# A decoder layer in one-level Strassen products: left operands made when their own products come up, branch operands fetched one by one

## The chip, the core and the metric

One core of a Trainium2 chip runs the whole kernel. TensorE (PE) multiplies, VectorE (DVE), ScalarE (ACT) and GpSimd (POOL) do elementwise work, SyncE (SP) issues most DMA transfers. The metric is the device time of one execution in microseconds (us); lower is better. Before the change the median of three runs is 2201.9 us (2199.32 to 2203.22).

## What is computed

One layer on a residual stream h of 1024 tokens by 1024 channels, float32:

```python
f = _swiglu(_rmsnorm(h, ffn1_pre_g), ffn1_w_gate, ffn1_w_up, ffn1_w_down)   # 1024 -> 2816 -> 1024
h = h + 0.5 * _rmsnorm(f, ffn1_post_g)
z = _rmsnorm(h, mix_pre_g) @ w_in                                          # u | v | c | ga | gb
a = u * (causal 128x128 token mixing of layernorm(v))                      # spatial gating unit
b = _pool_mixer(c, pool_w, pool_scale)                                     # trailing means, 4 windows
y = sigmoid(ga) * (a @ w_out_a) + sigmoid(gb) * (b @ w_out_b)
h = h + _rmsnorm(y @ w_o, mix_post_g)
f = _swiglu(_rmsnorm(h, ffn2_pre_g), ffn2_w_gate, ffn2_w_up, ffn2_w_down)
h = h + 0.5 * _rmsnorm(f, ffn2_post_g)
gate = sigmoid(_rmsnorm(h, ple_pre_g) @ ple_w_gate)
h = h + _rmsnorm(gate * (p @ ple_w_proj), ple_post_g)
```

## The kernel before

**Numbers.** A float32 product is done as three products of rounded halves: `split` (L127) makes a high half with a cast on ACT (L128) and a low half with a subtraction on DVE (L129); `mm3` (L134) issues low x high (L136), high x low (L137) and high x high (L138). One matmul instruction is 128x128 by 128x512.

**Strassen.** Every large product is cut into 2x2 blocks and done with seven products instead of eight, in the order p1, p2, p5, p6, p3, p7, p4. Left operands 0 and 1 (for p1, p2) are plain blocks; 2 to 6 are sums of blocks or the block a22. `Seven` (L167) holds a left operand's seven versions; `put` splits one piece into its place, `sums` (L177) makes operands 2, 6 and 3 in a step `first` and 5 and 4 in a step `second`, with half tiles from a pool of four (`half`, L99) for its intermediate sums. `feed` (L197) does this from normalised rows: tokens t = 0 to 3 give operands 0 and 1 (`early`), tokens 4 to 7 the rest (`late`), each after eight transposes on TensorE (L209). `FromDram` and `SumsFromDram` (L238, L273) read a left operand, or its ready sums, from DRAM.

**Stages**, in order: projection of p (to 49 us); first FFN's gate and up products (to 479), its down product (to 709); v of the mixer with its token mixing (to 812); u and c (to 985); gates, with the pooling products among them (to 1155); branch a (to 1233); branch b (to 1312); output projection (to 1401); second FFN (1412 to 2081); gate of the layer embedding, PLE (to 2181); final norm and output. `Columns` (L400) runs the groups of output columns, `Rows` (L485) the products whose output is by tokens, `ffn_down` (L644) the down products. `Columns` with `lead` = 2 runs p1 and p2 of the first two groups ahead of everything else, since operands 0 and 1 are ready first; then each group's other products. Weights come through `Right` (L334), made three steps ahead. Raw tiles from DRAM come from a pool of six (`raw`), full tiles from a pool of eleven (`full`).

**Order of side work.** `Later` (L39) is a queue of postponed steps with keys and costs: after each half product `allow(us)` pops steps while credit lasts; `flush` pops all. `closing` (L678) finishes a product's rows: squares on ACT (L149), scale on POOL (L143, L144), residual on DVE (L704), a second norm (L159), and then `feed`. `down_sums` (L572) makes sums of the next down product's weights in half tiles and stores them; `weight_sums` (L807) does that for the mixer's output weights, beside the first down product (`beside`). `sgu_constants` (L844) loads, masks (L852, on POOL) and transposes (L858) the token weights in the mixer's v stage. Branch outputs are multiplied by their gates and summed in DRAM: a's are written to `y_d`, b's are added there by an accumulating DMA from POOL's queue (L1067), and the output projection reads `y_d` as its left operand. The Tile framework's scheduler sets the final order of each engine's instructions from the order of the program and its own estimates; engines then run their rows in that order.

Of the kernel before, what the change touches and what calls it, by code (L numbers as in the profile page):

```python
# [38 lines left out]
class Later:  # L39

    def __init__(self):
        self.queue, self.credit, self.count = [], 0.0, 0

    def add(self, key, cost, step):
        heapq.heappush(self.queue, (key, self.count, cost, step))
        self.count += 1

    def allow(self, us):  # L50
        self.credit = min(self.credit + us, us)
        while self.queue and self.credit > 0:
            self.pop()

    def pop(self):
        _, _, cost, step = heapq.heappop(self.queue)
        self.credit -= cost
        step()

    def flush(self):  # L60
        while self.queue:
            self.pop()
# [3 lines left out]
def layer_kernel(ctx: ExitStack, tc: tile.TileContext, a: dict, out: bass.AP):  # L66
# [46 lines left out]
    ga_d, gb_d, c_d = (scratch(s, KD) for s in ("ga_", "gb_", "c_"))  # L113
    b_d, y_d = (dr.tile([P, KD, T], F32, name=s, tag=s) for s in ("b_d", "y_d"))
    as_d = scratch("a_s", 7, KD // 2 * HT)

    tw_d = {s: [scratch(f"{s}_t{h}", 4) for h in range(2)] for s in ("w_out_a", "w_out_b", "w_o")}
    sv_d = dr.tile([P, KD, T], F32, name="sv_d", tag="sv_d")
# [47 lines left out]

    class Seven:  # L167
        def __init__(self):
            self.op, self.kept = [None] * 7, {}

        def put(self, i, k, cols, src, e=nc.vector):
            if self.op[i] is None:
                self.op[i] = X([2, 4, HT], FR)
            o = self.op[i]
            split(o[:, 0, k, cols], o[:, 1, k, cols], src, e)

        def sums(self, k, cols, a11, a12, a21, a22, tmp):  # L177

            s2 = tmp()

            def first():
                s1 = tmp()
                nc.vector.tensor_tensor(s1, a22, a21, op=ALU.subtract)
                self.put(2, k, cols, s1)
                self.put(6, k, cols, a22)
                nc.vector.scalar_tensor_tensor(s2, a11, -1.0, s1, op0=ALU.mult, op1=ALU.subtract)
                self.put(3, k, cols, s2)

            def second():
                nc.vector.tensor_tensor(a21, a11, a21, op=ALU.subtract)  # L190
                self.put(5, k, cols, a21, nc.vector)
                nc.vector.scalar_tensor_tensor(s2, a12, -1.0, s2, op0=ALU.mult, op1=ALU.subtract)
                self.put(4, k, cols, s2)

            return first, second

        def feed(self, src, t, key):  # L197
# [3 lines left out]
            state = []  # L201
# [18 lines left out]
            def tmp():  # L220
                return half().rearrange("p (j t) -> p j t", j=4)

            def late():
                banks = transposed()
                a21 = tmp()
                nc.scalar.copy(a21, banks[0])
                a1, a2 = self.kept[t - 4][:, 0], self.kept[t - 4][:, 1]
                first, second = self.sums(k, cols, a1, a2, a21, banks[1], tmp)
                first()
                state.append(second)  # L230

            if t < 4:
                later.add(key, 1.4, early)
            else:
                later.add(key, 3.5, late)
                later.add(key, 2.8, lambda: state.pop()())

    class FromDram(Seven):  # L238
# [11 lines left out]
        def early(self):  # L250
            for kk in range(2):
                for i in range(2):
                    self.put(i, slice(2 * kk, 2 * kk + 2), slice(0, HT), self.block(0, i, kk))

        def late(self, kks, key):
            def one(kk):
                state = []

                def begin():
                    a11, a12, a21, a22 = (self.block(r, c, kk) for r in range(2) for c in range(2))  # L260
                    first, second = self.sums(
                        slice(2 * kk, 2 * kk + 2), slice(0, HT), a11, a12, a21, a22, lambda: full((2, HT))
                    )
                    first()
                    state.append(second)

                later.add(key, 6.2, begin)
                later.add(key, 4.9, lambda: state.pop()())

            for kk in kks:  # L270
                one(kk)

    class SumsFromDram(Seven):  # L273


        def __init__(self, src):
            Seven.__init__(self)
            self.src = src

        def load(self, i, kk):  # L280
            t = raw([2, HT])
            nc.sync.dma_start(t, self.src[i][:, kk * D:(kk + 1) * D].rearrange("p (k t) -> p k t", k=2))
            self.put(i, slice(2 * kk, 2 * kk + 2), slice(0, HT), t)

        def early(self):
            for i in range(2):
                for kk in range(2):
                    self.load(i, kk)

        def late(self, key):  # L290
            for i in range(2, 7):
                for kk in range(2):
# [870 lines left out]
```

## Time and profile before

| | |
|---|---|
| median of three runs | 2201.9 us |
| the profiled execution | 2197.74 us |
| its span | 2196.0 us |
| TensorE clock, mean | 0.975 of full |
| DMA | 421.67 MB, mean 192 GB/s |
| VectorE instructions | 1773 |
| GpSimd's queue (accumulating DMA) | 2304 packets, 4.20 MB |

A row of a profile view names line, engine, operation and tiles, `out<-in`; brackets hold the idle time ahead of it on its engine and what ended it. Lines are those of the kernel before. In the views, "x" is a count of instructions.

### The profile page before, as it was taken

What the parts mean: (1) busy time and instruction counts of PE and PEld (TensorE: products, weight loads), DVE (VectorE), ACT (ScalarE), POOL (GpSimd) and SP (SyncE); (2) the same over time, 40 slices, a digit from 0 to 9 for tenths busy, and PEclk for the clock granted to TensorE, in tenths of its full rate; (3) what the DMA queues carried; (4) which work ended last, traced back from release to release, by engine and by line L of the source; (5) the groups of instructions that cost most, each with busy time, mean ns of one, the idle gap of its engine ahead of it and who ended that gap; (6) DMA issues with size and microseconds to landing.
All of it is one profiled execution on the core that took longest, in us unless ns stands there. A gap on an engine that the chain in (4) does not pass through costs nothing. (4 is left out here: it accounts for less than half of the span.)

```text
span 2196.0 us, 25524 instructions
## 1 busy us (share of the span) xinstructions
PE 2084.6 (95%) x9228; PEld 1718.0 (78%) x9228; DVE 1472.1 (67%) x1773; ACT 944.0 (43%) x1359; POOL 141.8 (6%) x224
## 2 busy tenths in 40 slices
PE   7899999999999999999999998679999999999985
PEld 6688888888877788888788886568888888888774
DVE  6756666686575896567665757876666667545586
ACT  7433333344265633335454435643333334444463
POOL 2000000000012110000000012300000000001112
PEclk9999999999999999999999999889999999999998
DMA  8453545489866236445468887544354456764635
GB/s 286 141 172 120 190 137 168 158 306 385 357 223 203 73 111 203 138 154 161 133 227 296 271 229 225 197 141 162 135 169 157 146 180 225 230 194 164 205 118 192
DMA packets 300622, 421.67 MB, mean 192 GB/s; under 512 B 20048, under 2 KB 176720, under 8 KB 300496
## 3 DMA queue, kind: packets, MB, share of 16 engines
q1 hardware_dynamic: 298192, 415.84, 56.2%
q0 software_dynamic: 2304, 4.20, 1.2%
q8 instruction: 73, 1.20, 0.2%
q14 instruction: 53, 0.43, 0.1%
HBM read 286.27 MB, written 133.69 MB: 191 GB/s over the span
## 5 line engine op out<-in xcount | busy, mean ns | idle before, releaser
L136 PE MATMUL ps<-X,wt 128*128 128x512 f32 x1904 | 744.9, 392 | 22.9 <-ACT X L128 17.5
L137 PE MATMUL ps<-X,wt 128*128 128x512 f32 x1904 | 745.0, 391 | 1.9 <-DVE X L129 1.9
L138 PE MATMUL ps<-X,wt 128*128 128x512 f32 x1904 | 742.3, 391 | 0.0
L129 DVE TENSOR_TENSOR wt<-raw,wt 128x1024 fp32r<-128x1024 f32 x282 | 344.4, 1222 | 231.1 <-ACT wt L128 230.9
L136 PEld LDWEIGHTS ps<-X,wt 128*128 128x128 f32 x1904 | 359.8, 189 | 99.7 <-ACT X L128 18.6
L137 PEld LDWEIGHTS ps<-X,wt 128*128 128x128 f32 x1904 | 359.8, 189 | 78.0 <-DVE X L129 3.3
L138 PEld LDWEIGHTS ps<-X,wt 128*128 128x128 f32 x1904 | 359.8, 189 | 75.0
L128 ACT CAST wt<-raw 128x1024 fp32r<-128x1024 f32 x282 | 295.7, 1050 | 276.2 <-PE ps L138 158.1
L129 DVE TENSOR_TENSOR X<-raw,X 128x1024 fp32r<-128x1024 f32 (+1 forms) x198 | 222.3, 1146 | 148.4 <-ACT X L128 142.4
L128 ACT CAST X<-raw 128x1024 fp32r<-128x1024 f32 (+1 forms) x198 | 190.9, 992 | 177.0 <-PE ps L138 40.2
L136 PE MATMUL ps<-X 128*128 128x512 f32 x616 | 236.2, 394 | 9.1 <-ACT X L128 9.0
L137 PE MATMUL ps<-X 128*128 128x512 f32 x616 | 241.9, 393 | 1.3 <-DVE X L129 1.3
L138 PE MATMUL ps<-X 128*128 128x512 f32 x616 | 240.7, 392 | 0.0
L132 DVE TENSOR_TENSOR raw<-raw 128x1024 f32<-128x1024 f32 x136 | 165.9, 1222 | 9.9 <-DMA raw<-in_ple_w_gate_dram 3.0
L136 PE MATMUL ps<-wt,X 128*128 128x512 f32 x336 | 134.0, 412 | 12.5 <-ACT wt L128 9.4
L136 PEld LDWEIGHTS ps<-X 128*128 128x128 f32 x616 | 116.7, 190 | 34.6 <-ACT X L128 10.4
L137 PE MATMUL ps<-wt,X 128*128 128x512 f32 x336 | 135.4, 403 | 4.4 <-DVE wt L129 4.4
L137 PEld LDWEIGHTS ps<-X 128*128 128x128 f32 x616 | 116.8, 190 | 26.4 <-DVE X L129 2.2
L138 PEld LDWEIGHTS ps<-X 128*128 128x128 f32 x616 | 116.8, 190 | 24.4
L138 PE MATMUL ps<-wt,X 128*128 128x512 f32 x336 | 134.2, 400 | 0.0
L323 ACT ACTIVATE f<-ps 128x512 f32<-128x512 f32 x88 | 52.3, 598 | 126.0 <-PE ps L138 126.0
L321 ACT ACTIVATE f<-ps 128x512 f32<-128x512 f32 x88 | 52.4, 598 | 100.3 <-PE ps L138 96.4
(128 smaller groups left out, 1863.3 us busy)
## 6 DMA issues: line engine op xcount, KB each, us to landing
raw<-ffn_s SPq DMA_DIRECT2D x70, 512.0 KB, 5.2
raw<-in_ffn_w_gate_dram SPq DMA_DIRECT2D x96, 256.0 KB, 4.1
raw<-in_ffn_w_up_dram SPq DMA_DIRECT2D x96, 256.0 KB, 4.6
f<-in_ffn_w_down_dram SPq DMA_DIRECT2D x44, 512.0 KB, 4.9
ffn_t<-hf SPq DMA_DIRECT2D x88, 256.0 KB, 4.8
ffn_s<-hf SPq DMA_DIRECT2D x88, 256.0 KB, 4.9
raw<-ffn_t SPq DMA_DIRECT2D x40, 512.0 KB, 4.8
ffn_s<-f SPq DMA_DIRECT2D x66, 256.0 KB, 2.0
```

The source lines that it names most:

```text
L128: nc.scalar.copy(hi, src)
L129: e.tensor_tensor(lo, src, hi.bitcast(F32), op=ALU.subtract)
L132: e.tensor_tensor(dst, u, v, op=ALU.add)
L136: nc.tensor.matmul(ps, wl[1], wr[0], start=first, stop=False, skip_group_check=True)
L137: nc.tensor.matmul(ps, wl[0], wr[1], start=False, stop=False, skip_group_check=True)
L138: nc.tensor.matmul(ps, wl[0], wr[0], start=False, stop=last, skip_group_check=True)
L321: nc.scalar.activation(at("22"), y, AF.Copy, scale=-1.0)
L323: nc.scalar.activation(at("12"), x, AF.Copy, scale=-1.0)
```

## The change

Left operands 3, 4 and 5 are no longer made with 2 and 6. The arithmetic and the splits for p6, p3 and p7 are bound to their product and forced only when that product comes up (`before`, `meet`, `need`); until then they run when credit allows. The sums are made in place, in tiles kept anyway and in one more operand tile (`rest`), not in half tiles:

```diff
+    def before(self, product, cost, step):
+        self.due.append((product, self.count, 0, cost, step))
...
+    def meet(self, product):
+        while self.due and self.due[0][0] <= product:
+            self.pop(self.due)
...
-        def sums(self, k, cols, a11, a12, a21, a22, tmp):
...
+        def sums(self, k, cols, a11, a12, a21, a22, s1, us):
+            nc.vector.tensor_tensor(s1, a22, a21, op=ALU.subtract)
+            self.put(2, k, cols, s1)
+            self.put(6, k, cols, a22)
+
+            def others():
+                nc.vector.scalar_tensor_tensor(s1, a11, -1.0, s1, op0=ALU.mult, op1=ALU.subtract)
+                self.put(3, k, cols, s1)
+                nc.vector.scalar_tensor_tensor(a12, a12, -1.0, s1, op0=ALU.mult, op1=ALU.subtract)
+                nc.vector.tensor_tensor(a11, a11, a21, op=ALU.subtract)
+
+            later.before(self.base + 3, 4 * us, others)
+            later.before(self.base + 4, us, lambda: self.put(4, k, cols, a12))
+            later.before(self.base + 5, us, lambda: self.put(5, k, cols, a11))
...
-                a21 = tmp()
+                if t == 4:
+                    self.rest = X([2, 4, HT], F32)
+                a21, s1 = (self.rest[:, i, :, cols] for i in range(2))
```

Both branches read ready sums, one operand (two loads of 512 KB) at a time, started in the last products of the stage ahead; b's sums are now made where the pooling products end, and both branches run without `lead`. Gates are read and multiplied two blocks at a time; in b's second group a's part of y is loaded and added on DVE, and two blocks of y go into the output projection's operands straight from SBUF:

```diff
+        def fetch(self):
+            i, self.fetched = self.fetched, self.fetched + 1
+            for kk in range(2):
+                t = raw([2, HT])
+                nc.sync.dma_start(t, self.src[i][:, kk * D:(kk + 1) * D].rearrange("p (k t) -> p k t", k=2))
...
+    def last_a(i):
+        if i >= 2:
+            left_b.fetch()
+        if i == 6:
+            b_cols.right.ahead(2)
...
+    def done_b(g, key, where, o):
+        if g == 0:
+            nc.gpsimd.dma_start(y_d[:, where[0], where[1]], o, accum_op=ALU.add)
+            return
+        ya = raw([2, HT])
+        nc.sync.dma_start(ya, y_d[:, where[0], where[1]])
+        add(o, o, ya)
...
+    def last_b(i):
+        if i == 4:
+            ysum.early(0)
+        if i == 5:
+            o_rows.right.ahead(1)
+        if i == 6:
+            later.add(0, 3.7, lambda: ysum.late(0))
```

Other work is placed elsewhere: the token weights are masked and transposed in the projection of p, stored and read back (`token_weights`); `down_sums` runs after a group instead of ahead of it; the next stage's loads start at p4 of a down product instead of p7; the sums of the mixer's output weights are spread over its first five products; closing norms may wait a few half products; and weights are made two steps ahead, not three, in the first three steps of an FFN:

```diff
+    def token_weights():
+        ws, turned = half(), half()
+        w = ws.rearrange("p (g s) -> p g s", g=SGU_G)
+        nc.sync.dma_start(w, a["sgu_w"][0].rearrange("g t s -> t g s"))
...
+        nc.sync.dma_start(ws_d, turned)
...
-            if i == 5:
-                last()
...
-                if kp % 2 == 0 and beside:
+                if beside and (kp == 1 or (i, kp) == (0, 3)):
                     beside.pop(0)()
+
             rest = [right.get(i * PAIRS + kp) for kp in range(outer, PAIRS)]
+            if i == 6:
+                last()
...
-            later.add(t + 1, 1.3, norm)
-            left.feed(hp, t, t + 2)
+            later.add(t + 1, 1.3, norm, 1)
+            left.feed(hp, t, t + 2, max(3, t))
...
-            self.right = Right(make, self.steps, 3)
+            self.right = Right(make, self.steps, lambda s: LOOK if s < 2 * lead - 1 else 3)
...
-            self.right = Right(lambda i: make(i, state, (True, False)), list(range(7)), 1)
+            self.right = Right(lambda i: make(i, state, (False, False)), list(range(7)), 1)
```

How this moves instructions, at three places. (Rows are line, operation, `out<-in` with tile numbers, and shape. In the changed kernel `split` is L147 and L148, the norm L178, the sums L207 to L215, the residual L730.)

VectorE ahead of the first FFN's first p5, whose left operand is X_514 and whose weight is wt_762. Before:

```order
L192 SCALAR_TENSOR_TENSOR hf_745<-f_418,hf_745 128x512
L132 TENSOR_TENSOR f_853<-f_853,ps_901 128x512
L129 TENSOR_TENSOR wt_917<-raw_758,wt_917 128x1024
L132 TENSOR_TENSOR hf_834<-hf_831,f_826 128x512
L132 TENSOR_TENSOR hf_837<-f_824,f_826 128x512
L605 TENSOR_TENSOR f_822<-f_822,f_853 128x512
L129 TENSOR_TENSOR X_561<-hf_745,X_561 128x4x128
L183 TENSOR_TENSOR hf_868<-ps_860,hf_865 128x512
L190 TENSOR_TENSOR hf_865<-f_459,hf_865 128x512
L186 SCALAR_TENSOR_TENSOR hf_867<-f_459,hf_868 128x512
L129 TENSOR_TENSOR X_514<-hf_868,X_514 128x4x128
```

After, where the same operand is X_513, its last piece is written here, and 67 matmul rows follow before p5 reads it:

```order
L212 SCALAR_TENSOR_TENSOR X_510<-f_419,X_510 128x4x128
L148 TENSOR_TENSOR wt_732<-raw_729,wt_732 128x1024
L148 TENSOR_TENSOR X_513<-X_510,X_513 128x4x128
L214 SCALAR_TENSOR_TENSOR f_355<-f_355,X_510 128x512
L215 TENSOR_TENSOR f_355<-f_355,X_510 128x512
L148 TENSOR_TENSOR X_516<-ps_653,X_516 128x4x128
```

The last token's difference (L183), the two sums behind it and the sums of down weights (hf_834, hf_837) stood ahead of the operand's last piece; now one weight and another token's scaled sum do.

VectorE between token 5's residual (L704, L730) and its normalised row (L159, L178), in the seam from the output projection to the second FFN. Before:

```order
L704 SCALAR_TENSOR_TENSOR f_10166<-f_10166,sc_10641,raw_10638 128x1024
L692 TENSOR_TENSOR f_10181<-ps_9980,f_10052 128x512
L192 SCALAR_TENSOR_TENSOR hf_10609<-f_10312,hf_10609 128x512
L129 TENSOR_TENSOR wt_10800<-raw_10793,wt_10800 128x1024
L704 SCALAR_TENSOR_TENSOR f_10181<-f_10181,sc_10663,raw_10660 128x1024
L132 TENSOR_TENSOR hf_10736<-f_10732 128x512
L129 TENSOR_TENSOR X_10679<-hf_10609,X_10679 128x4x128
L159 SCALAR_TENSOR_TENSOR raw_10638<-f_10166,sc_10671,f_10054 128x1024
```

After:

```order
L730 SCALAR_TENSOR_TENSOR f_10107<-f_10107,sc_10578,raw_10575 128x1024
L207 TENSOR_TENSOR X_10653<-ps_10648,X_10653 128x4x128
L151 TENSOR_TENSOR raw_10774<-raw_10774,raw_10777 128x1024
L148 TENSOR_TENSOR X_10656<-X_10653,X_10656 128x4x128
L178 SCALAR_TENSOR_TENSOR raw_10575<-f_10107,sc_10586,f_10001 128x1024
```

Token 6's residual, token 4's last sum and split and a down-weight sum are gone from between; a weight sum and token 4's operand 2 stand there.

SyncE's loads from branch b's end into the output projection (`y_d` is the gated sum, `gb_d` the gates, `in_w_o` and `w_o_t` the weights of the output projection). Before:

```order
L247 DMA raw_9895<-y_d_138 128x2x512
L247 DMA raw_9897<-y_d_138 128x2x512
L247 DMA raw_9899<-y_d_138 128x2x512
L247 DMA raw_9901<-y_d_138 128x2x512
L501 DMA raw_9932<-in_w_o_dram 128x2x512
L501 DMA raw_9934<-in_w_o_dram 128x2x512
L247 DMA raw_9995<-y_d_138 128x2x512
L247 DMA raw_9997<-y_d_138 128x2x512
L247 DMA raw_9999<-y_d_138 128x2x512
L247 DMA raw_10001<-y_d_138 128x2x512
L493 DMA raw_10028<-w_o_t00_162 128x1024
```

After:

```order
L1097 DMA raw_9863<-gb_d_130 128x2x512
L266 DMA raw_9867<-y_d_131 128x2x512
L266 DMA raw_9869<-y_d_131 128x2x512
L266 DMA raw_9871<-y_d_131 128x2x512
L266 DMA raw_9873<-y_d_131 128x2x512
L1121 DMA raw_9896<-y_d_131 128x2x512
L522 DMA raw_9899<-in_w_o_dram 128x2x512
L522 DMA raw_9901<-in_w_o_dram 128x2x512
L514 DMA raw_9975<-w_o_t00_162 128x1024
```

The weights of p2 (the first two rows of `in_w_o`) stood behind four loads of y; now behind five and a load of gates, and the next weights directly follow.

More of the change, by code (lines that the diff above doesn't have):

```diff
@@ L164, in gain @@
         return g
+    ALL = slice(0, HT)
+    count = [0]
     class Seven:
@@ L248, in block, with early, late @@
             return out
[L250 to L271, printed above, removed]
+        def early(self, kk):
+            for i in range(2):
+                self.put(i, slice(2 * kk, 2 * kk + 2), ALL, self.block(0, i, kk))
+        def late(self, kk):
+            a21, a22, a11, a12 = (self.block(r, c, kk) for r in (1, 0) for c in range(2))
+            self.sums(slice(2 * kk, 2 * kk + 2), ALL, a11, a12, a21, a22, full((2, HT)), 1.3)
     class SumsFromDram(Seven):
@@ L277, in __init__, with need @@
             Seven.__init__(self)
[L278 to L292, printed above, removed]
-                    later.add(key, 1.3, lambda i=i, kk=kk: self.load(i, kk))
+            self.src, self.fetched = src, 0
+        def fetch(self):
[3 more added lines that the diff above has]
+                nc.sync.dma_start(t, self.src[i][:, kk * D:(kk + 1) * D].rearrange("p (k t) -> p k t", k=2))
+                k = slice(2 * kk, 2 * kk + 2)
+                later.before(self.base + i, 1.3, lambda t=t, k=k: self.put(i, k, ALL, t))
+            later.first = True
+        def need(self, i):
+            if self.fetched < 7:
+                self.fetch()
+            later.meet(self.base + i)
     def pairs():
@@ L305, in pairs, with packed, places, at @@
         return at
+    def packed():
+        tiles = {}
+        def places(n):
+            def at(key):
+                if key not in tiles:
+                    tiles[key] = full((2, HT))
+                return tiles[key][:, n, :]
+            return at
+        return tiles, places(0), places(1)
     class Out:
@@ L342, in get @@
         def get(self, s):
[L343 removed]
+            self.ahead(s + 1 + self.look(s))
             out, self.done[s] = self.done[s], None
@@ L605, in up @@
                 nc.vector.tensor_tensor(g[key], g[key], src, op=ALU.mult)
-            return [Out(gate, places), Out(up)]
+            return [Out(gate, places), Out(up, others)]
         def after(c):
             spill(hid.pop(c), lambda i: s_d[s][i][:, c * HT:(c + 1) * HT])
+            if c < HC - 1:
+                down_sums(c)
+            if c == HC - 2:
+                down_sums(c + 1)
             if c == HC - 1:
                 later.flush()
-        cols.run(left, outs, after, last)
+        cols.run(left, outs, after, lambda i: last() if i == 6 else None)
     PAIRS, TAIL = (HC + 1) // 2, 2
@@ L943, in uc_outs @@
         return [Out(u_final, u_places), Out(c_final, c_places)]
-    uc_cols.run(left, uc_outs, lambda g: None, lambda: gate_cols.right.ahead(2), 5)
+    uc_cols.run(left, uc_outs, lambda g: None, lambda i: gate_cols.right.ahead(2) if i == 6 else None, 5)
     later.flush()
@@ L1012, in products @@
             w, blk = state["w"], 2 * gi + b
+            both = full((2, HT))
             for h in range(2):
@@ L1073, in layer_kernel, with branch, outs, one @@
-    o_rows = Rows(a["w_o"][0], tw_d["w_o"])
-    def last_a():
-        b_cols.right.ahead(2)
-        left_b.early()
-    def last_b():
-        o_rows.right.ahead(1)
-        ysum.early()
-        ysum.late((0,), 0)
-    a_cols.run(left_a, outs_a, lambda g: None, last_a)
-    left_b.late((0, 1), 0)
-    b_cols.run(left_b, outs_b, lambda g: None, last_b)
-    ysum.late((1,), 0)
+    gate_cols.run(left, gate_outs, lambda g: None, gate_last, 25, 1.0)
+    def branch(gates, done):
+        def outs(g):
+            tiles, *places = packed()
+            gts = {}
+            def one(n):
+                def f(key, src):
+                    h, c = int(key[0]) - 1, int(key[1]) - 1
+                    where = (slice(4 * c + 2 * g, 4 * c + 2 * g + 2), slice(h * HT, (h + 1) * HT))
+                    if n == 0:
+                        gts[key] = raw([2, HT])
+                        nc.sync.dma_start(gts[key], gates[:, where[0], where[1]])
+                    if key == "21":
+                        nc.vector.tensor_tensor(places[n](key), src, gts[key][:, n], op=ALU.mult)
+                    elif n == 1:
+                        nc.vector.tensor_tensor(tiles[key], tiles[key], gts[key], op=ALU.mult)
+                    if n == 1:
+                        done(g, key, where, tiles[key])
+                return Out(f, places[n])
+            return [one(0), one(1)]
+        return outs
@@ L1090, in layer_kernel @@
+    later.add(0, 3.7, lambda: ysum.sums(slice(2, 4), ALL, *(tops[i] for i in range(4)), full((2, HT)), 1.3))
     h2_cols = hidden_weights("ffn2")
```

179 lines of the change are left out of this document (85 added, 94 removed).

## The prediction

> **What bounds the kernel now.** I read the profile's page first, then TensorE's waits, then stretches of time, then single stretches of the timeline.
>
> ```profile
> PE 2084.6 (95%) x9228; PEld 1718.0 (78%) x9228; DVE 1472.1 (67%) x1773; ACT 944.0 (43%) x1359; POOL 141.8 (6%) x224
> PE   7899999999999999999999998679999999999985
> PEclk9999999999999999999999999889999999999998
> ```
>
> TensorE is busy for 95% of the span, so at most 111 us of idle time can go (2196.0 - 2084.6), plus what a lowered clock costs. Both sit in few places: the slices of 54.9 us that aren't 9 are the first two, the 25th to 27th (1318 to 1482 us, from the mixer's output projection into the second FFN) and the last two. What stands before TensorE there:
>
> ```profile
> PE ps L136 <- ACT X L128: 26.5, 5, 9.1
> PE ps L209 <- DVE raw L159: 25.8, 8, 8.6
> PE ps L136 <- ACT wt L128: 10.2, 5, 4.1
> PE ps L858 <- POOL hf L852: 2.9, 1, 2.9
> ```
>
> (us in all, times, longest.) Three quarters are waits for a left operand's high half (L128 into X), for the normalised rows that are transposed (L159 before L209), or for a weight. None of it is a shortage over the whole span: VectorE (DVE) has 67%. It is order, at seams where VectorE has norms, operand sums and weights to do at once. By stretches:
>
> ```profile
> 60.00:100.00 40.00, 29.13 (x118) 22.84 (x117) 28.34 (x40) 17.31 (x26) 0.00 (x0) 0.87 0.46 151
> 200.00:250.00 50.00, 50.00 (x222) 41.42 (x221) 31.45 (x37) 16.85 (x22) 0.00 (x0) 1.00 0.42 137
> 1300.00:1350.00 50.00, 42.75 (x166) 33.74 (x165) 36.68 (x40) 20.73 (x29) 10.23 (x9) 0.90 0.88 250
> 1400.00:1470.00 70.00, 41.59 (x174) 33.47 (x173) 59.89 (x80) 35.69 (x64) 13.61 (x19) 0.78 0.54 179
> 2075.00:2120.00 45.00, 37.47 (x170) 29.76 (x169) 39.62 (x51) 26.47 (x49) 14.50 (x18) 0.96 0.38 128
> 814.00:817.00 3.00, 3.00 (x11) 2.61 (x11) 2.83 (x9) 2.07 (x2) 0.00 (x0) 0.50 0.66 198
> ```
>
> (Length, then busy time and count of PE, PEld, DVE, ACT, POOL, then granted clock, DMA share, GB/s.) The undisturbed stretch from 200 on gives the price of a 128x512 matmul: 50.00/222 = 0.225 us. By it the 118 rows of 60 to 100 are worth at most 26.6 us; there are 10.9 us of idle time and at least 2.6 us of slow clock. In 1400 to 1470, 28.4 us are idle and at least 2.4 us (41.59 - 174 x 0.225) go to the clock, while VectorE is busy for 86%.
>
> **The change, part by part.** Instruction counts on PE and VectorE are the same in both programs, so this is a change of places. I used one tool for all parts: between two rows of TensorE's order I added the VectorE rows at the distance from start to start of these
>
> ```profile
> 1456.17 0.68 DVE L129 TENSOR_TENSOR X<-hf,X 128x512 fp32r<-128x512 f32 x1
> 1456.77 0.68 DVE L129 TENSOR_TENSOR X<-ps,X 128x512 fp32r<-128x512 f32 x1
> L129 DVE TENSOR_TENSOR wt<-raw,wt 128x1024 fp32r<-128x1024 f32 x282 | 344.4, 1222 | 231.1 <-ACT wt L128 230.9
> L128 ACT CAST wt<-raw 128x1024 fp32r<-128x1024 f32 x282 | 295.7, 1050 | 276.2 <-PE ps L138 158.1
> ```
>
> (0.60 us for 512 columns; for 1024 the 1.22 shown less the same overlap, 1.14), and compared with 24 matmuls, 5.4 us. What VectorE has above TensorE in such a slice I call its excess. Checked on before: 9.9 us of excess ahead of the first p5, against 10.9 idle; 36.4 in the seam of 1400 to 1470, against 28.4. So it finds the places, and overstates seams by about a fifth.
>
> *1. Operand sums late (first FFN).* Now the p5 product waits for the last token's operands:
>
> ```profile
> 83.39 1.22 PE L136 MATMUL ps<-X,wt 128*128 128x512 f32 x2 [8.37 <-ACT X L128]
> 84.03 0.69 DVE L186 SCALAR_TENSOR_TENSOR hf<-f,hf 128x512 f32<-128x512 f32 x1 [0.62 <-DMA ffn_t<-hf]
> ```
>
> and L186 itself waits for a half tile that a transfer to `ffn_t` holds. In the order of after, operand 2 is complete 67 matmul rows (15 us) ahead of p5, there are no half tiles in the way, and the sums of down weights stand behind the group. The 10.9 us and 2.6 us go: -13.5. Late next: the transposes of tokens 6 and 7 are moved up among the projections of p, where the slices carry 4.5 us more excess than before. Net **-9** (from -13.5 to -3).
>
> *2. Same part at the second FFN, with the closing norm's order.* Here are three long waits and one chain:
>
> ```profile
> 1411.07 1.94 PE L209 MATMUL ps<-ident,raw 128*128 128x128 f32 x8 [8.56 <-DVE raw L159]
> 1427.77 1.94 PE L209 MATMUL ps<-ident,raw 128*128 128x128 f32 x8 [8.44 <-DVE raw L159]
> 1459.36 1.22 PE L136 MATMUL ps<-X,wt 128*128 128x512 f32 x2 [9.10 <-ACT X L128]
> 1419.88 1.28 DVE L704 SCALAR_TENSOR_TENSOR f<-f,sc,raw 128x1024 f32<-128x1024 f32 x1
> 1421.19 1.06 ACT L149 ACTIVATE raw<-f 128x1024 f32<-128x1024 f32 x1 [0.77 <-DVE f L704]
> 1423.63 2.67 POOL L144 TENSOR_TENSOR sc<-sc,nhalf 128x1 f32<-128x1 f32 x1
> 1426.34 1.29 DVE L159 SCALAR_TENSOR_TENSOR raw<-f,sc 128x1024 f32<-128x1024 f32 x1 [0.44 <-POOL sc L144]
> ```
>
> From token 5's residual (L704) to its transposes (1427.77) is a chain of 7.9 us that no order shortens below its own steps. What the order changes is when L704 starts: before, it stands behind ten VectorE rows, most of them sums and splits of token 4; after, it is the first row behind token 4's transposes. Excess of the seam falls from 36.4 to 21.9; scaled by 28.4/36.4 that is -11.3, and I add -1 for slow clock. **-12** (from 0, if the chain binds in all four tokens, to -25).
>
> *3. The next norm's seam (PLE).* Same rules, but there the excess rises from 13.0 to 17.7. The stretch 2075 to 2120 has 7.5 us idle; 4.7 x 7.5/13.0 = **+3** (-3 to +6).
>
> *4. Token weights.*
>
> ```profile
> 729.77 1.30 POOL L852 TENSOR_SCALAR_AFFINE_SELECT hf<-hf 128x512 f32<-128x512 f32 x1 [0.25 <-DMA hf<-in_sgu_w_dram]
> 731.12 0.66 PE L858 MATMUL ps<-ident,hf 128*128 128x128 f32 x4 [2.90 <-POOL hf L852]
> ```
>
> Both move to the prologue, behind a norm that TensorE waits for anyway; later only a load remains, beside other work. **-3** (-4 to 0). If that cover isn't there, the 1.3 us of the select are paid at the start.
>
> *5. The down products' ends.*
>
> ```profile
> 661.83 2.08 PE L136 MATMUL ps<-X 128*128 128x512 f32 x4 [4.13 <-ACT X L128]
> 2033.93 2.07 PE L136 MATMUL ps<-X 128*128 128x512 f32 x4 [3.86 <-ACT X L128]
> 605.32 0.51 PE L136 MATMUL ps<-X 128*128 128x512 f32 x1 [1.01 <-ACT X L128]
> 606.58 0.50 PE L137 MATMUL ps<-X 128*128 128x512 f32 x1 [0.75 <-DVE X L129]
> 609.15 0.50 PE L137 MATMUL ps<-X 128*128 128x512 f32 x1 [0.58 <-DVE X L129]
> ```
>
> The first two are p7's operands, with the next stage's loads ahead of them on SP's queue; those loads now stand after p4's. The last three follow a stretch in which the sums for `w_o` and the branches' weights share the DMA with down's operands; they are spread over five products now. Gone: 8.0 + 2.3, and 2 of slow clock. New: 3.9 us of excess where p4 begins in the first down product, 3.1 more than before in the second; if they are paid in full, 7. **-5** (-10 to +5).
>
> *6. Branches and output projection.* Operands one by one: in the order each load is issued at least 28 us ahead of its product, against 6.1 us to land, so the fetches cost nothing; what hides them is the five products (5.4 us each) that run between an operand's load and its use. The first weight of a and of b is issued only 6.3 us ahead:
>
> ```profile
> raw<-a_s SPq DMA_DIRECT2D x14, 512.0 KB, 6.1
> raw<-in_w_o_dram SPq DMA_DIRECT2D x6, 512.0 KB, 5.8
> raw<-in_w_out_a_dram SPq DMA_DIRECT2D x6, 512.0 KB, 4.9
> 1324.65 1.20 PE L136 MATMUL ps<-wt,X 128*128 128x512 f32 x4 [3.66 <-ACT wt L128]
> 1066.30 0.64 PE L136 MATMUL ps<-X,wt 128*128 128x512 f32 x1 [2.43 <-DVE wt L129]
> ```
>
> it needs 4.9 + 1.05 + 1.22 = 7.2, so 0.9 of wait, twice, for the 2.4 us of 1066. In the output projection before, a weight issued 3.4 us (15 matmul rows) ahead waited 3.66; 1300 to 1350 has 7.25 us idle. After, p2's weight is issued only 1.8 us (8 rows) ahead, because gate and `y` tiles hold the raw buffers: 5.8 + 1.05 - 1.8 = 5 us, then two lesser waits of 1 to 2.5 us. **0** (-6 to +6).
>
> Sum: -9 - 12 + 3 - 3 - 5 + 0 = **-26 us**, against the profiled execution, 2197.7 us (span 2196.0): 2171.7. The median of the runs, 2201.9, is 4.2 us above that execution; on its scale the sum gives **2176**.
>
> The slow clock counts in two of these terms, and the trace shows it after short waits too:
>
> ```profile
> 811.72 0.33 PE L136 MATMUL ps<-f,raw 128*128 128x128 f32 x1 [1.84 <-DVE raw L886]
> ```
>
> after 1.84 us of idle time the stretch 814 to 817 ran at 0.50. [...]
>
> **Rivals.**
> - *The norm's chain binds* (chance 0.15). The four tokens' transposes wait 7.9 us each whatever VectorE does between; part 2 gives 0, and the output projection's late weights cost 4. For it: L159 ends just before both transposes. Against: before L704 VectorE was never free. -26 + 12 + 4 = -10: 2192.
> - *The waits move from p5 to p6; slower* (0.11). Four VectorE rows per token (0.69 each in 512 columns, 2.75) are now due when p6 comes up; five operands are made so, four tokens each: 5 x 4 x 2.75 = 55 us. It decides where VectorE is still behind when p5 ends, since p6's steps are then forced in one block that p5's 5.4 us can't hide. In full: -26 + 55 = +29: 2231; half of it still ends at 2204. For it: in the order at the second FFN p6's last operand is finished right before p6. Against: at the first FFN it stands some 50 rows ahead.
> - *It does nothing measurable* (0.06): gains of parts 1 and 2 are given back at p4 of down and at PLE; 2200.
> - *All seams clear* (0.10): parts 1 to 5 at their good ends, -45 or more: 2157.
>
> **How the numbers follow.** The forecast has 0.58; its own range is 2160 to 2193, from the parts' bounds taken as independent. For 8 in 10 the range takes in the first and third rival, the better end of "all seams clear", and the milder half of p6's: **2150 to 2206**. A measurement of this kernel tells 0.2% (4.4 us) from no change. Faster by more: 0.58 less a little, 0.10 and most of 0.15: 0.78. Within: 0.09. Slower: 0.13.
>
> **What would show it.** Part 1: no wait over 2 us ahead of the first p5. Part 2: 1400 to 1470's counterpart with some 17 us idle, not 28. Part 4: no wait for the select. Part 5: no 4 us at p7's operands. Part 6: a wait of about 5 us for p2's weight in the output projection. Wrong if p6, p3 or p7 products wait for X in the FFNs, or if branch products wait for their operands' loads.

## The result, and the profile after

| | before | after |
|---|---|---|
| median of four runs | 2202.4 us | 2148.3 us |
| range | 2199.3 to 2203.2 | 2148.0 to 2153.8 |
| profiled execution, its span | 2197.7, 2196.0 | 2153.8, 2151.7 |

Ratio of after to before: 0.9763, 95% interval 0.9744 to 0.9781, so 48 to 56 us less. The forecast was 26, and the median lies 1.7 us below the lower end of the range given with it (2150 to 2206). The profile of after is of its slowest run: its span is 44.3 us shorter than that of before, its three other runs were another 5.5 us shorter.

The page of after, the lines shown of before:

```profile
PE 2070.9 (96%) x9228; PEld 1712.7 (80%) x9228; DVE 1472.0 (68%) x1773; ACT 939.9 (44%) x1360; POOL 141.0 (7%) x212
PE   7999999999999799999999999989999999999986
PEclk9999999999999899999999999999999999999988
```

VectorE has the same work (1472.1 before). TensorE's busy time fell by 13.7 us for the same matmuls (its mean clock rose from 0.975 to 0.983), and its idle time by 30.6. The slices at 1318 to 1482 us are nines but one; one slice has become worse, the 14th (700 to 750 us). TensorE's waits of after:

```profile
PE ps L232 <- DVE raw L178: 35.3, 11, 7.2
PE ps L155 <- DVE f L345: 4.7, 3, 2.4
PE ps L155 <- ACT X L147: 2.6, 1, 2.6
PE ps L156 <- DVE wt L148: 2.3, 4, 1.0
PE ps L155 <- ACT wt L147: 0.8, 1, 0.8
```

Waits for a left operand's high half have gone from 26.5 to 2.6 us, those for a weight's cast from 10.2 to 0.8. Waits of transposes for the normalised rows (L232 for L178) have grown from 25.8 to 35.3. By stretches, in the columns used above: the first FFN's first products, the output projection, the seam into the second FFN, the seam into PLE, and the one into v:

```profile
60.00:100.00 40.00, 40.00 (x178) 33.15 (x177) 34.28 (x44) 21.64 (x31) 0.00 (x0) 1.00 0.34 105
1276.00:1326.00 50.00, 48.80 (x215) 39.76 (x214) 41.31 (x42) 25.41 (x35) 2.00 (x2) 1.00 0.75 251
1375.00:1445.00 70.00, 57.41 (x242) 46.44 (x241) 62.19 (x79) 39.27 (x66) 10.07 (x15) 0.88 0.42 132
2030.00:2075.00 45.00, 32.59 (x139) 26.08 (x138) 38.81 (x51) 25.44 (x48) 12.69 (x16) 0.85 0.41 141
695.00:735.00 40.00, 27.77 (x114) 22.48 (x113) 34.22 (x45) 21.69 (x38) 10.08 (x10) 0.83 0.38 118
```

The first is full, with 178 matmuls where before had 118 in it. The output projection's idle time went from 7.25 to 1.2 us, that of the FFN's seam from 28.4 to 12.6, but PLE's rose from 7.5 to 12.4.

To compare whole stages I took, in both traces, the time from the m-th to the n-th of the 9228 recorded matmuls. Both programs have the same number of matmuls in nearly the same order, so I take a difference in such a stretch as that stage's gain:

| stretch (matmuls) | term of the prediction | forecast | before to after | measured |
|---|---|---|---|---|
| first FFN's start (60 to 300) | 1 | -9 | 70.6 to 56.4 | -14.2 |
| into the second FFN (5760 to 6240) | 2 | -12 | 137.4 to 121.6 | -15.8 |
| into PLE (8760 to 9060) | 3 | +3 | 74.9 to 82.0 | +7.1 |
| v stage (2880 to 3180, 3180 to 3600) | 4 | -3 | 74.4 to 82.2, 80.0 to 76.3 | +4.1 |
| down products (2500 to 2640, 2640 to 2880, 8580 to 8700) | 5 | -5 | 35.3 to 31.7, 57.6 to 58.6, 30.1 to 23.5 | -9.2 |
| gates to a (4560 to 5040), b into output projection (5640 to 5760) | 6 | 0 | 115.3 to 114.9, 39.6 to 29.0 | -11.0 |
| PLE's end (9060 to 9227) | none | 0 | 48.2 to 40.3 | -7.9 |

They add up to -46.9; behind the last matmul after takes 2.8 us longer.

Each value is from one profile. Between seams the profiles agree closely (matmuls 300 to 2500 take 498.7 us in all of them), but at the seams they scatter, and the profile of after is on the slow side: its 114.9 us for gates to a holds a wait of 2.4 us with a granted clock of 0.50 behind it, and the eleven edits of the changed kernel below take 110.9 to 112.9 there. Where a difference of a few us matters below, the spread over the runs is given.

### The profile page after: what moved, and what is told of

Same layout as the page of the kernel before. It is cut to its first block, busy times and chain, and to the rows that moved or that the text cites. A ratio compares the mean times of both kernels' runs of the same rounds, so it can differ in the third digit from the quotient of the medians.

```text
span 2151.7 us, 25497 instructions
## 1 busy us (share of the span) xinstructions
PE 2070.9 (96%) x9228; PEld 1712.7 (80%) x9228; DVE 1472.0 (68%) x1773; ACT 939.9 (44%) x1360; POOL 141.0 (7%) x212
## 5 line engine op out<-in xcount | busy, mean ns | idle before, releaser
L148 DVE TENSOR_TENSOR wt<-raw,wt 128x1024 fp32r<-128x1024 f32 x282 | 343.5, 1220 | 235.0 <-ACT wt L147 234.9
L147 ACT CAST wt<-raw 128x1024 fp32r<-128x1024 f32 x282 | 295.5, 1050 | 268.7 <-PE ps L157 129.2
L148 DVE TENSOR_TENSOR X<-raw,X 128x1024 fp32r<-128x1024 f32 (+1 forms) x201 | 224.0, 1145 | 113.6 <-ACT X L147 113.1
L147 ACT CAST X<-raw 128x1024 fp32r<-128x1024 f32 (+1 forms) x201 | 192.1, 993 | 156.2 <-PE ps L157 66.6
L156 PE MATMUL ps<-wt,X 128*128 128x512 f32 x336 | 133.8, 398 | 1.8 <-DVE wt L148 1.8
L155 PE MATMUL ps<-wt,X 128*128 128x512 f32 x336 | 132.1, 401 | 1.2 <-DVE f L345 1.2
L157 PE MATMUL ps<-wt,X 128*128 128x512 f32 x336 | 133.0, 396 | 0.0
L340 ACT ACTIVATE f<-ps 128x512 f32<-128x512 f32 x88 | 52.6, 598 | 122.5 <-PE ps L157 122.3
```

Of the source, the lines that this page charges most:

```text
L147: nc.scalar.copy(hi, src)
L148: e.tensor_tensor(lo, src, hi.bitcast(F32), op=ALU.subtract)
L155: nc.tensor.matmul(ps, wl[1], wr[0], start=first, stop=False, skip_group_check=True)
L156: nc.tensor.matmul(ps, wl[0], wr[1], start=False, stop=False, skip_group_check=True)
L157: nc.tensor.matmul(ps, wl[0], wr[0], start=False, stop=last, skip_group_check=True)
L340: nc.scalar.activation(at("12"), x, AF.Copy, scale=-1.0)
```

## The experiments

Each is an edit of the changed kernel or of the one before, timed against before on the same chip. "Ratio" is to before throughout; the changed kernel's is 0.9763 (0.9744 to 0.9781).

**Are the late operands what pays?** The changed kernel with operands made at once:

```diff
-            later.before(self.base + 3, 4 * us, others)
-            later.before(self.base + 4, us, lambda: self.put(4, k, cols, a12))
-            later.before(self.base + 5, us, lambda: self.put(5, k, cols, a11))
+            others()
+            self.put(4, k, cols, a12)
+            if cols is ALL:
+                self.put(5, k, cols, a11)
+                return
+            self.last5 = getattr(self, "last5", []) + [lambda: self.put(5, k, cols, a11)]
+            if len(self.last5) == 4:
+                for step in self.last5:
+                    step()
...
-                later.add(key, 2.1, late, wait)
+                later.add(key, 6.3, late, wait)
```

> The changed kernel, but operands 3 and 4 and their sums are made at once with 2 and 6 again (operand 5 with the last token's), in place as in the change. If the lateness of the sums pays (terms 1 and 2 of the prediction, -13 and -16 us in the trace): waits of 6 us or more come back ahead of p5 in both FFNs, and the time rises by 15 to 30 us over the changed kernel, to 2163-2178. If it is the half tiles and the moved sums of down weights that cleared p5: no wait over 3 us ahead of p5, 2146-2154.

Measured: 2148.3 us, ratio 0.9760 (0.9741 to 0.9778). With the other parts of the change in place, lateness, which gives the change its name, is worth nothing in the total that could be told from zero (the intervals leave some 6 us either way). Ahead of the first p5 there is no wait, as in the stretch of 60 to 100 us:

```profile
60.00:100.00 40.00, 40.00 (x183) 33.20 (x182) 35.16 (x45) 19.09 (x29) 0.00 (x0) 1.00 0.31 95
```

It isn't that nothing moves. At once, the seam into v (matmuls 2880 to 3180) takes 75.9 us instead of 82.2 (77.8 to 82.2 in the ten runs with late sums there) and the one into PLE 78.1 instead of 82.0 (78.5 to 82.1 in nine runs), but the rest of the v stage (3180 to 3600) takes 85.7 instead of 76.3 (76.3 to 76.4 in the ten), with waits of 1.5 and 2.8 us for the centred rows of v, and the seam into the second FFN 122.6 instead of 121.6. Gains and losses cancel.

**Is it the sums of down weights?** The kernel before, with this one part of the change:

```diff
-            later.add(0, 1.4, first)
-            later.add(0, 1.4, lambda: state.pop()())
+            later.add(90, 1.4, first)
+            later.add(91, 1.4, lambda: state.pop()())
...
-            down_sums(c)
...
+            if c < HC - 1:
+                down_sums(c)
+            if c == HC - 2:
+                down_sums(c + 1)
```

> The kernel before, with one part of the change: the sums of the next down product's weights run after a group instead of ahead of it. If half tiles held by their transfers delayed the operand sums: the 8.4 us wait ahead of the first p5 falls below 4, and the time falls by 5 to 15 us, to 2187-2197. If the operand sums themselves are too much for VectorE there: the wait stays over 6, and the time stays within 4 us of 2202.

Measured: 2180.5 us, ratio 0.9912 (0.9896 to 0.9929), 19 us less: more than either theory allowed for. The first p5's wait hasn't halved, it has gone, with the operand sums, the half tiles and everything else as before:

```profile
60.00:100.00 40.00, 40.00 (x183) 33.20 (x182) 32.91 (x42) 18.65 (x26) 0.00 (x0) 1.00 0.29 90
```

Matmuls 60 to 300 take 56.1 us (70.6 before, 56.4 changed), so this part is the whole of term 1. The seam into the second FFN goes from 137.4 to 133.0, with the two waits of transposes still there and the one of 9.1 us for operands cut to two of 2.2:

```profile
1397.13 1.09 PE L209 MATMUL ps<-ident,raw 128*128 128x128 f32 x4 [8.75 <-DVE raw L159]
1412.31 1.09 PE L209 MATMUL ps<-ident,raw 128*128 128x128 f32 x4 [9.71 <-DVE raw L159]
1439.02 0.73 PE L136 MATMUL ps<-X,wt 128*128 128x512 f32 x2 [2.24 <-ACT X L128]
```

Whether VectorE's rows or the half tiles held by their stores mattered more isn't separated: the edit moves both.

**Does y's trip through DRAM cost anything?** The changed kernel with both groups of b added in DRAM and loaded from there:

```diff
-        if g == 0:
-            nc.gpsimd.dma_start(y_d[:, where[0], where[1]], o, accum_op=ALU.add)
-            return
+        nc.gpsimd.dma_start(y_d[:, where[0], where[1]], o, accum_op=ALU.add)
+        return
...
             later.add(0, 3.7, lambda: ysum.late(0))
+            ysum.early(1)
...
-    later.add(0, 3.7, lambda: ysum.sums(slice(2, 4), ALL, *(tops[i] for i in range(4)), full((2, HT)), 1.3))
+    later.add(0, 3.7, lambda: ysum.late(1))
```

> The changed kernel, but both groups of branch b are added to y in DRAM by the accumulating DMA, and the second half of the output projection's operands is loaded from there. If it is this trip through DRAM whose loads stood ahead of the weights on SyncE's queue (the changed kernel's output projection has 10.6 us less than before): waits of 3 us or more for weights or operands come back at p2 to p6 of the output projection, +7 to +12 us, 2155-2160. If the trip is hidden and the gain came from elsewhere: within 3 us of the changed kernel's 2148.

Measured: 2160.0 us, ratio 0.9818 (0.9802 to 0.9833), 12 us of loss, at the upper end of the range expected and at the place expected: matmuls 5640 to 5760 take 42.7 us (29.0 in the changed kernel, 39.6 before). In the timeline, SyncE's issues, GpSimd's accumulating DMA and TensorE's waits:

```profile
1294.59 2.13 SPq L266 DMA_DIRECT2D raw<-y_d  x4
1299.71 6.89 SPq L522 DMA_DIRECT2D raw<-in_w_o_dram  x2
1306.62 1.22 POOL L1117 DMA_DIRECT2D y_d<-f  x1 [11.55 <-DVE f L1099]
1309.35 2.08 PE L155 MATMUL ps<-wt,X 128*128 128x512 f32 x4 [6.86 <-ACT wt L147]
1313.80 0.80 PE L156 MATMUL ps<-wt,X 128*128 128x512 f32 x1 [2.38 <-DVE wt L148]
```

Four loads of y stand ahead of the weights, and the two weight loads take 6.9 us to be issued; p2 waits 6.86 us, where before the change it waited 3.66. In the changed kernel, the same weights:

```profile
1301.54 2.64 SPq L522 DMA_DIRECT2D raw<-in_w_o_dram  x2
1305.35 1.05 ACT L147 CAST wt<-raw 128x1024 fp32r<-128x1024 f32 x1 [1.96 <-DMA raw<-in_w_o_dram]
1309.51 0.50 PE L156 MATMUL ps<-wt,X 128*128 128x512 f32 x1 [1.02 <-DVE wt L148]
```

The load is issued 5.9 us ahead of p2 (its first matmul starts at 1307.4), lands within 3.8, and p2 waits 1.0.

**What did the down products' ends wait for?** Two edits of the changed kernel, first apart:

```diff
+            if i == 5:
+                last()
...
-            if i == 6:
-                last()
```

> The changed kernel, but a down product starts the next stage's loads at p7 again, not at p4. If these loads, ahead of p7's operands on SyncE's queue, were what p7 waited for (term 5: 4.1 and 3.9 us of idle time, with the slow clock some 6 us each): both waits come back and the 3 us wait now at p4 of the first down product goes, +6 to +12 us, 2154-2160. If p7 waited for work of VectorE and ScalarE that the change moved otherwise: within 3 us of 2148.

```diff
-            self.right = Right(lambda i: make(i, state, (False, False)), list(range(7)), 1)
+            self.right = Right(lambda i: make(i, state, (True, False)), list(range(7)), 1)
```

> The changed kernel, but in products by rows the first weight block is kept for p5, as before, not loaded twice. Before, the layer embedding's gate product waited 4.1 and 3.2 us for weights near its end; changed, 1.2 and 0.6. If the kept block held two of six raw buffers and so delayed later loads: these waits come back, +4 to +9 us, 2152-2157. If loads or stores elsewhere freed the buffers: within 3 us.

Measured: 2148.2 us (0.9769, 0.9752 to 0.9786) and 2148.9 us (0.9771, 0.9754 to 0.9789). Neither can be told from the changed kernel, and p7's wait stays away in both. Then both:

> The changed kernel with both: the next stage's loads at p7 of a down product, and the first weight block of a product by rows kept for p5. Each alone changed nothing. Before, the kept block held two of six raw buffers from p7 on, and p7's operands waited. If the two together starved p7 of buffers: the wait at p7 of the second down product (3.9 us, 6 with the slow clock) comes back, and the layer embedding's late waits for weights too, +6 to +14 us, 2154-2162. If not: within 3 us of 2148, and the cause stays open.

Measured: 2167.2 us, ratio 0.9847 (0.9833 to 0.9861), 19 us more than the changed kernel. The wait at p7 of the second down product is back with 3.9 us, the same as before the change; the first now waits 15.6:

```profile
635.47 0.43 SPq L522 DMA_DIRECT2D raw<-in_w_in_dram  x1
636.85 0.32 SPq L664 DMA_DIRECT2D raw<-ffn_s  x1
642.34 2.64 SPq L865 DMA_DIRECT2D f<-in_w_o_dram  x3
645.08 0.48 SPq L664 DMA_DIRECT2D raw<-ffn_t  x1
654.63 1.04 ACT L147 CAST X<-raw 128x1024 fp32r<-128x1024 f32 x1 [11.54 <-DMA raw<-ffn_t]
655.73 1.65 PE L155 MATMUL ps<-X 128*128 128x512 f32 x3 [15.56 <-ACT X L147]
```

The operand's two halves (`ffn_s`, `ffn_t`) are issued 8.2 us apart, behind a weight of the next stage and with loads and stores for the sums of `w_o` between them. Matmuls 2640 to 2880 take 13.3 us more than in the changed kernel and 8580 to 8700 take 5.7 more: all of the loss. With the loads at p7 alone the pair goes out next to each other:

```profile
635.73 0.43 SPq L664 DMA_DIRECT2D raw<-ffn_t  x1
636.49 0.43 SPq L664 DMA_DIRECT2D raw<-ffn_s  x1
637.62 0.32 SPq L664 DMA_DIRECT2D raw<-ffn_t  x1
```

So it takes both, and either remedy is enough. Why is argued, not shown: a block kept for p5 and loaded that early holds two of six raw buffers while down's operands still need them. Before the change that shows in the first down product, where half of an operand (`ffn_t`, issued at 656.85) waits 2.7 us on SyncE until transposes, which read raw tiles, are done. In this run the halves' own waits on SyncE are only 0.9 and 0.4 us; there the order of the queue, with the next stage's weights ahead, may do the rest. PLE's late waits for weights did not come back (no wait over 1 us behind 2083 us), so that part of the expectation fell.

**Norm waits and flush in pieces.** Removed everywhere, and then kept for the output projection's closing only:

```diff
+                if i == 2:
+                    later.flush()
                 for t in range(4):
-                    if i == 2:
-                        later.flush(t + 6 if t < 3 else None)
...
-            later.add(t + 1, 1.3, norm, 1)
-            left.feed(hp, t, t + 2, max(3, t))
+            later.add(t + 1, 1.3, norm)
+            left.feed(hp, t, t + 2)
```

> The changed kernel, but the closing norms and transposes have no least wait, and a product by rows flushes its whole queue at once at p5, as before. If these waits shaped the seam into the second FFN (28.4 us idle before, 13 after): that seam loses 5 us or more, and the time rises by 4 to 12 us, to 2152-2160. If the late sums alone did it: the seam stays within 3 us; and if the waits are what made the seam into v worse (5.9 us idle before, 12.9 after), that seam gets 4 us or more better, 2140-2148.

Measured: 2150.6 us, ratio 0.9774 (0.9759 to 0.9790). The seam into the second FFN loses 5.0 us (121.6 to 126.6 for matmuls 5760 to 6240), as expected, v's and PLE's gain 2.2 and 3.5, and the total stays below the 2152 to 2160 expected. Then, with the waits and pieces behind a flag that only that closing sets:

> The changed kernel with the norms' least waits and the flush in pieces kept only where they helped, at the output projection's closing; the closings of both down products have none and products by rows flush at once. By the run without any waits, the seams into v and into the layer embedding gain some 2 and 4 us, and the seam into the second FFN keeps its 5: 2140-2145, faster than the changed kernel. If what that run showed was the spread of one profile: 2146-2152.

Measured: 2148.6 us, ratio 0.9767 (0.9747 to 0.9788). The gain did not come: the seam took 124.8 us all the same, though its closing's waits were the changed kernel's. Seven edits that leave this closing and its late sums as they were took 120.5 to 122.3 us there, so 3 us are not scatter: what happens at this seam depends on edits elsewhere too, by a path that I did not follow.

**Weights two steps ahead.** Three again (`LOOK = 3`):

> The changed kernel with weights made three steps ahead in an FFN's first steps, as before, instead of two. The seam into the second FFN gained 15.6 us; late sums and the norms' waits account for at most 6 of it by the runs so far. If the third weight's sum and split on VectorE stood in the norm's way there: the seam loses 3 us or more, 2151-2156. If not: within 2 us.

Measured: 2145.9 us, ratio 0.9755 (0.9737 to 0.9773): not told from the changed kernel.

**All three together**, sums at once, no waits, three steps:

> The changed kernel with three things of the seam into the second FFN undone together: sums made at once, no least waits and one flush, weights three steps ahead. One at a time they moved that seam by -1, -5 and 0 us, of the 11 that the moved sums of down weights leave unexplained. If they stand in for each other: the seam loses 8 us or more, and the time rises by 6 to 14 us, 2154-2162. If what is left comes from the half tiles that no sum uses any more: at most 5 us there, 2146-2153.

Measured: 2144.4 us, ratio 0.9745 (0.9732 to 0.9758). They don't stand in for each other: the seam into the second FFN takes 123.7 us against 121.6, and the total is lower than either case expected. The seam into v takes 73.1 against 82.2, of which the rest of that stage gives 6.8 back (83.1 against 76.3), and PLE's 78.4 against 82.0. In windows of the same length as above, the seams into v and into the second FFN:

```profile
690.00:730.00 40.00, 34.17 (x155) 27.07 (x154) 35.43 (x45) 22.75 (x41) 12.19 (x13) 0.96 0.39 125
1372.00:1442.00 70.00, 53.01 (x232) 43.13 (x233) 61.46 (x80) 37.86 (x64) 13.37 (x16) 0.90 0.41 128
```

At v 5.8 us are idle, where the changed kernel has 12.2; at the FFN 17.0, where it has 12.6 and before had 28.4.

**The output weights' sums and the token weights**, put back where they were (two edits, read in different stretches):

```diff
-                if beside and (kp == 1 or (i, kp) == (0, 3)):
+                if beside and kp % 2 == 0:
...
-            if (j, t) == (1, 6):
-                token_weights()
...
-        nc.sync.dma_start(ws, ws_d.rearrange("p (g s) -> p g s", g=SGU_G))
-        split(ws_t[:, 0], ws_t[:, 1], ws)
+        nc.sync.dma_start(ws, a["sgu_w"][0].rearrange("g t s -> t g s"))
+        nc.gpsimd.affine_select(
+            out=ws, in_=ws, pattern=[[0, SGU_G], [-1, P]], compare_op=ALU.is_ge, fill=0.0,
+            base=0, channel_multiplier=1,
+        )
...
+            nc.tensor.transpose(ps[:, gi * P:(gi + 1) * P], ws[:, gi, :], ident)
```

> The changed kernel with two parts undone that touch different stretches: the output weights' sums beside the first three products of the first down product, and the token weights masked and transposed in the v stage. Term 5: 2.3 us of waits and slow clock at 590-600 come back (3.6 us in the changed kernel's favour so far), and the 4.0 us of waits at p4 (655) go: within 4 us. Term 4: a wait of 2 to 3 us for the select comes back at the v stage. If the select's wait had only hidden another: no wait for it, or the next wait shorter by as much. In all 2145-2153.

Measured: 2151.9 us, ratio 0.9780 (0.9766 to 0.9793). The sums beside three products cost 9.8 us in matmuls 2500 to 2640 (41.5 against 31.7) and give 7.9 back in 2640 to 2880 (50.7 against 58.6), where p4 now waits for nothing: net some 2 us. No wait for the select came back at v, so in the changed order it is not what ends last there: the transposes still wait for their rows, 2.4, 2.9 and 5.5 us. The start took 4.0 us longer (60.4 against 56.4).

**A try at a faster kernel**: sums at once for PLE's left operand alone, weights three steps ahead.

> A try at a faster kernel: the changed one, with sums at once for the layer embedding's left operand alone, and weights three steps ahead in an FFN's first steps. Sums at once gained 3 to 4 us in that seam's stretch, three steps ahead 0 to 2: 2142-2146. If those were the spread of single profiles: 2146-2150.

Measured: 2145.3 us, ratio 0.9749 (0.9736 to 0.9763). This one and the three parts undone have the lowest times of all, but their intervals overlap with the changed kernel's; a faster kernel is not shown.

## Why the prediction was right in its direction and half in its size

The sum of the parts hides how they came out. Parts 1 to 5 were forecast at -26 and measured -28.0, but each was off by 4 to 7 us, two up and three down, so that agreement is luck. "All seams clear", the rival nearest in size, is not what happened either: it needed -45 from these five parts, and two seams got longer. What the sum lacked lies in part 6 and in a stretch for which it had no term.

*Term 1, the first p5.* Forecast -9, measured -14.2. The wait went as said. The moved sums of down weights are shown to be enough by themselves, and the late sums, which I named first, not to be needed. The 4.5 us that I gave back for transposes among p's projections were not paid: the one wait there that is new is 0.6 us.

*Term 2, the seam into the second FFN.* Forecast -12, measured -15.8: mis-sized by 3.8. Which part brings it is not settled. Sums of down weights bring 4.4 of it (137.4 to 133.0), late sums, waits and two steps together 2.1 (123.7 to 121.6). If the effects add, the remaining 9.3 lie in parts that I did not take apart: sums in place instead of in half tiles, and FFN tiles in pairs. y's path through DRAM is not among them (120.5 with it). The earlier residual that I forecast for token 5 is in the trace of after:

```profile
1382.85 1.97 PE L232 MATMUL ps<-ident,raw 128*128 128x128 f32 x8 [4.61 <-DVE raw L178]
1384.73 1.28 DVE L730 SCALAR_TENSOR_TENSOR f<-f,sc,raw 128x1024 f32<-128x1024 f32 x1 [0.20 <-POOL sc L163]
1389.49 1.28 DVE L178 SCALAR_TENSOR_TENSOR raw<-f,sc 128x1024 f32<-128x1024 f32 x1
```

It starts 1.9 us behind the start of token 4's transposes, where before it was 8.8 (1411.07 to 1419.88), and the wait of 8.4 us for token 5 is gone; tokens 6 and 7 wait 4.6 and 2.5 in its place. In the kernel before with down's sums moved, the residual still stands 8.75 us behind and the wait is 9.7. So this step came out as forecast; which edit moves the residual no run separates.

*Term 3, PLE.* +3 was +7.1, of the right sign. Late sums are part of it: at once the stretch takes 78.1 to 78.4 in three runs, late 78.5 to 82.1 in nine. The moved sums of down weights may be another: with them alone it takes 77.7, 2.8 more than before. Not foreseen is PLE's end, -7.9. These two waits of before

```profile
2163.82 2.08 PE L136 MATMUL ps<-wt,X 128*128 128x512 f32 x4 [4.12 <-ACT wt L128]
2169.13 0.79 PE L137 MATMUL ps<-wt,X 128*128 128x512 f32 x1 [3.23 <-DVE wt L129]
```

are 1.2 and 0.6 us now, and no edit of the changed kernel brought them back, so the cause stays open.

*Term 4, token weights.* -3 failed: the select's wait of 2.9 us is gone, and the stage took 4.1 us more (0 to 4 more over the ten runs with late sums). The transposes' own waits grew, from 0.7 and 2.0 to 3.1, 2.6 and 6.6 us. The seam lost 7.8 us, of which 6.3 go when sums are made at once; the rest of the stage gained 3.7. With the select out of the way and the sums at once the seam still takes 75.9 us against 74.4 before, so the select's removal by itself bought nothing there. The transposes' waits before and after, and VectorE and GpSimd ahead of the longest:

```profile
717.35 1.09 PE L209 MATMUL ps<-ident,raw 128*128 128x128 f32 x8 [1.96 <-DVE raw L159]
```

```profile
711.71 1.97 PE L232 MATMUL ps<-ident,raw 128*128 128x128 f32 x8 [2.58 <-DVE raw L178]
726.45 1.97 PE L232 MATMUL ps<-ident,raw 128*128 128x128 f32 x8 [6.60 <-DVE raw L178]
```

```profile
719.39 2.86 POOL L162 TENSOR_SCALAR sc<-sc 128x1 f32<-128x1 f32 x1 [7.33 <-ACT raw L168]
722.33 0.55 POOL L163 TENSOR_TENSOR sc<-sc,nhalf 128x1 f32<-128x1 f32 x1
722.72 0.68 DVE L148 TENSOR_TENSOR X<-X 128x512 fp32r<-128x512 f32 x1
...
723.92 0.67 DVE L151 TENSOR_TENSOR f<-f,ps 128x512 f32<-128x512 f32 x1
724.52 0.68 DVE L148 TENSOR_TENSOR X<-f,X 128x512 fp32r<-128x512 f32 x1
...
725.12 1.27 DVE L178 SCALAR_TENSOR_TENSOR raw<-f,sc 128x1024 f32<-128x1024 f32 x1
```

The scale is done at 722.9 (L163), but L178 starts at 725.1, behind four rows of operands and sums, one of them the split of a late operand (`X<-f`, 724.52). That is 2.2 us of the wait, and the rival "the waits move" at another place than I gave it: not at p6, but at the next token's norm. Another 3.5 us are the scale itself on GpSimd (719.39 to 722.88), which takes 0.8 for token 5 at the second FFN (1387.28 to 1388.11); why it takes so long here no run shows.

*Term 5, down's ends.* -5 was -9.2. Later loads were said to free p7; it takes the kept block as well to block it, so not keeping it would have been enough. I had the queue and missed the kept block. Of the new wait at p4, 4.0 us were paid, as forecast for the first product; the second has none.

*Term 6, the output projection.* This is the step that failed most: "p2's weight is issued only 1.8 us (8 rows) ahead" and so a wait of 5 us. It was issued 5.9 us ahead, and p2 waited 1.0; the lesser waits forecast behind it, and the two of 0.9 us for the branches' first weights, were not paid either. I had read a lead in time out of the place of a load among the rows of another engine, and trusted it because the same reading met the 3.66 us of before. The order says what follows what on one queue; in this trace the time at which SyncE reached the load did not follow from the load's place among TensorE's rows. The -11 of this term (y through DRAM costs 12) and PLE's end, -7.9, are 18.9 of the 21 us that the forecast lacked.

The branches' operands, fetched one by one, came in time, as said.

## What to carry to other kernels

When a seam is full on one engine, look first for work in it that nothing near needs: moving the sums of the next product's weights out of the way gave 19 us by itself, while making the seam's own sums later added nothing to the other parts: what it won in one stretch it lost in others. A load's lead is the distance from its issue to its use on the chip (5.9 us for p2's weight, where its place among TensorE's rows had given 1.8); two programs' orders can be compared queue by queue, but not as clocks. And a buffer held for later and a load issued early can each be free alone and cost 19 us together, so undo suspects in pairs before calling them harmless.

## What the runs showed of the chip

The clock after a short wait did not follow from the wait's length alone. Before, 1.84 us of idle time were followed by a granted clock of 0.50; in after, a wait of 3.05 us was followed by 1.00, and one of 2.39 us by 0.50:

```profile
702.57 0.65 PE L232 MATMUL ps<-ident,raw 128*128 128x128 f32 x4 [3.05 <-DVE raw L178]
1131.82 0.79 PE L155 MATMUL ps<-X,wt 128*128 128x512 f32 x1 [2.39 <-DVE f L345]
```

The wait of 3.05 us is spread over two stretches of 3.4 us, in which TensorE was still busy for 46% and 65%; of the one of 2.39 us, 2.0 lie in one stretch of that length, 41% busy, and the next ran at 0.50:

```profile
697.95:701.36 3.41, 1.57 (x7) 0.95 (x6) 1.87 (x3) 0.71 (x2) 0.57 (x2) 1.00 0.15 59
701.36:704.78 3.42, 2.21 (x14) 2.00 (x15) 3.42 (x5) 1.03 (x2) 0.00 (x0) 1.00 0.07 4
1128.02:1131.44 3.42, 1.41 (x7) 0.83 (x5) 2.63 (x3) 3.42 (x5) 0.00 (x0) 1.00 0.31 112
1131.44:1134.85 3.41, 3.03 (x7) 2.45 (x8) 3.41 (x5) 2.46 (x4) 0.00 (x0) 0.50 1.01 247
```

Busy time as the profile shows it didn't decide every case either. Before, the stretch that holds the wait of 1.84 us was 64% busy, and the next ran at 0.50 all the same:

```profile
810.51:813.92 3.41, 2.20 (x20) 2.20 (x20) 3.41 (x4) 0.00 (x1) 0.13 (x1) 1.00 0.85 226
813.92:817.33 3.41, 3.41 (x13) 2.93 (x12) 3.24 (x11) 2.20 (x2) 0.21 (x2) 0.50 0.61 182
```

What decides it these rows don't show. So here the clock that a wait cost could not be told from its length: behind the 2.39 us stand 3.4 us at 0.50, behind the 3.05 us the clock stayed at 1.00 for 9 us.
